# Affine steps on the bare rows: from pairs between the stages to single steps beside the weight loads, pinned on GpSimd

## The chip, the cores and the metric

One core of a Trainium2 chip runs the whole program. The metric is device time in microseconds (us) of one execution. The core has TensorE (PE, with its weight loads as PEld), VectorE (DVE), ScalarE (ACT), GpSimd (POOL) and SyncE (SP), which here issues every DMA from one queue. Each engine takes its instructions in the order in which the program lists them; semaphores hold an instruction until what it reads is there and what it overwrites has been read.

## The reference, cut to what matters

Two layers (`DEPTH = 2`) of a transformer on 512 rows (plus 256 context rows, 768 in all) of 1024 numbers. Each layer is feed-forward, mixer, feed-forward, and each of these ends in a residual with a layer norm:

```python
def swiglu(h, wg, wu, wd):
    return (jax.nn.silu(h @ wg) * (h @ wu)) @ wd

def sublayer_in(h, m, i):
    return h * (1.0 + m[..., i, 1, :]) + m[..., i, 0, :]

def residual(h, sub, m, i, g, b):
    return layer_norm(DEEPNORM_ALPHA * h + (1.0 + m[..., i, 2, :]) * sub, g, b)
```

The last step of `layer_norm` is an affine one, times `g` and plus `b` for each column. The hidden width of the feed-forward is 2816, which the kernel cuts into eleven pairs of 128 columns.

## The kernel before

Four feed-forward stages run, called here by layer and place: (0,0), (0,2), (1,0) and (1,2), with a mixer after (0,0) and one after (1,0). All four are one function, `ffn` (L367 to L851). Stage (1,2) has 512 rows, the others 768.

**Pairs and groups.** The eleven pairs are taken in five groups, [0,1], [2,3], [4,5], [6,7], [8,9,10] (L365). For each pair there are gate and up products (tiles `pl`, `pc` at L574 for pairs done plainly, `ch` and `sd` at L512 for the others), the result `act` (L450, L451), and at the end of each group `down` (L712), which multiplies `act` with the down weights into PSUM tiles `pd` (L723), two of them in turn, one for each of the six row tiles. ScalarE copies the first group's `pd` to `acc` (L729); VectorE adds the later groups (L731). The last group is done by `down_last`.

**Weights.** `prepare` (L817) pops jobs from a list: `load(pr, q)` brings the gate (q=0) or up (q=1) weights of a pair, `prep_down(pr)` the down weights, 1 MB each, into two buffers `raw` (L345). Every 128x512 part is then split into two fp16 pieces, the high one by ScalarE (L331), the rest by VectorE (L332). In the stages with 768 rows, pairs from 2 on are multiplied in seven products instead of eight, and for this `load` first makes four sums of the raw weights on GpSimd, `S1` to `S4` (L427 to L430); these take three buffers in turn, so `S4` waits until `S1` has been split. The pieces lie in a ring of 21 blocks that TensorE's products free again. In `load` the splits stand in the order raw, raw, `S2`, `S3`, `S1`, `S4`, raw.

**Affine steps.** A layer norm whose result goes into a feed-forward stage (0,2), (1,0) or (1,2) stores only the rows without gain and bias (`row`, "bare rows"). The residual at the end of that stage needs them with both. `dress` (L741) is a generator that does this in steps: for each half of the columns it loads gain and bias (`gx`, `bx`, L750, L751), and for each row tile it loads a 128x512 piece of `row` (`xd`, L754), multiplies and adds on GpSimd (L755, L756) and stores the result as `xrow` (L757). Twelve steps in (0,2) and (1,0), eight in (1,2). The tiles come from four buffers `bc`, which the gates of the residual (L737) use later too. `xrow` is read at the end, in `residual` (L768).

**What sets the order.** The kernel is written in one stream; a scheduler with a timeline of its own then orders each engine's instructions, and may put one that it takes to be ready ahead of others that stand before it in the source. In the source two affine steps stand after the `prepare` of each of the pairs 2 to 7 (L841). `ada_vec` (L154) is other work between the products: 1 MB loads `adaw` with one buffer (L169) and 16 small matmuls for each (L164), four loads for each of the vectors that a stage has in its list (six in (0,0) and (0,2), four in (1,0), none in (1,2)).

Of the kernel before, what the change touches and what calls it, by code (L numbers as in the profile page):

```python
# [11 lines left out]
ALU = mybir.AluOpType  # L12
# [30 lines left out]
def kernel(  # L43
# [5 lines left out]
    out, stop=None, out_ctx=None,  # L49
):  # L50
    nc = tc.nc
    V, A, G, PE = nc.vector, nc.scalar, nc.gpsimd, nc.tensor
# [314 lines left out]
    def ffn(l, i, uT, stream, ntiles, nxt, last, todo):  # L367
# [5 lines left out]
        with tc.tile_pool(name=f"ffn{l}{i}", bufs=1) as fp:  # L373
# [103 lines left out]
            def input_differences():  # L477
                new_differences()
                for t in range(ntiles // 2):
                    u = []  # L480
                    for q in range(2):
                        u.append(ft("xa", [P, KC, P], f"u{l}{i}{t}{q}"))
                        tq = t + q * ntiles // 2
                        nc.sync.dma_start(out=u[q], in_=(stream.whole[:, :, tq * P:(tq + 1) * P] if start else
                                                         stream.inputs[tq]))
                    differences(u[0][:, 0:4], u[1][:, 0:4], u[0][:, 4:8], u[1][:, 4:8], slice(0, 4),
                                slice(t * P, (t + 1) * P), [P, 4, P], f"{t}")
# [220 lines left out]
            def new_acc():  # L708
                for t in range(ntiles):
                    acc[t] = ft("xa", [P, D], f"acc{l}{i}_{t}")  # L710

            def down(gi, prs):  # L712

                for t in range(ntiles):
                    hf, o = t // (ntiles // 2), (t % (ntiles // 2)) * P
                    pp = big([P, 2, 512], f"pd{l}{i}_{gi}{t}")
                    for h in range(2):
                        pd = pp[:, h]
                        n = 0
                        for q in prs:  # L720
                            for cc in range(2):
                                for a, b in PASSES:
                                    PE.matmul(pd, lhsT=acts[q][2 * cc + hf][:, a, o:o + P],  # L723
                                              rhs=wd[q][2 * cc + h][:, b],
                                              start=(n == 0), stop=(n == len(prs) * 6 - 1))
                                    n += 1
                    pp = pp.rearrange("p h f -> p (h f)")
                    if gi == 0:
                        A.copy(acc[t], pp)  # L729
                    else:  # L730
                        V.tensor_tensor(out=acc[t], in0=acc[t], in1=pp, op=ALU.add)  # L731
# [9 lines left out]
            def dress():  # L741

                n = 3 * stream.prev[0] + stream.prev[1]
                bare = dict(stream.rows)
                for t in range(ntiles):
                    stream.rows[t] = dram.tile([P, D], F32, name=f"xrow{l}{i}_{t}")
                for h in range(2):
                    sl = slice(h * 512, (h + 1) * 512)
                    g, b = (ft("bc", [P, 512], f"{nm}{l}{i}{h}") for nm in ("gx", "bx"))
                    nc.sync.dma_start(out=g, in_=agb[n, sl].partition_broadcast(P))  # L750
                    nc.sync.dma_start(out=b, in_=agb[6 + n, sl].partition_broadcast(P))  # L751
                    for t in range(ntiles):
                        xt = ft("bc", [P, 512], f"xd{l}{i}_{t}{h}")
                        nc.sync.dma_start(out=xt, in_=bare[t][:, sl])  # L754
                        G.tensor_tensor(out=xt, in0=xt, in1=g, op=ALU.mult)  # L755
                        G.tensor_tensor(out=xt, in0=xt, in1=b, op=ALU.add)  # L756
                        nc.sync.dma_start(out=stream.rows[t][:, sl], in_=xt)  # L757
                        yield

            dressing = dress() if stream.bare else None  # L760

            def residual(h):

                sl = slice(h * 512, (h + 1) * 512)
                gates = gate_rows_of(h)
                for t in range(ntiles):
                    xt = ft("pt", [P, 512], f"xt{l}{i}_{t}{h}")
                    nc.sync.dma_start(out=xt, in_=stream.rows[t][:, sl])  # L768
                    if stream.prev is None:
                        A.mul(xt, xt, ALPHA)  # L770
                    c_ = acc[t][:, sl]
                    G.tensor_tensor(out=c_, in0=c_, in1=gates[0 if t < NLT else 1], op=ALU.mult)  # L772
                    V.tensor_tensor(out=c_, in0=c_, in1=xt, op=ALU.add)
# [40 lines left out]
            def need(job):  # L814
                return 7 if job[0] == load and job[1] not in gu_plain else 4

            def prepare(used=0):  # L817

                ahead[0] -= used
                while jobs and ahead[0] + need(jobs[0]) <= NBLOCK + NEXTRA:  # L820
                    job = jobs.pop(0)
                    ahead[0] += need(job)
                    job[0](*job[1:])

            if start:
                finish = first_pair()
            else:
                load_plain(0)
            prepare()
            for gi, prs in enumerate(GROUPS):  # L830
                for q in prs:
                    if start and q == 0:
                        finish()
                    else:
                        (gate_up_plain if q in gu_plain else gate_up)(q)
                    if q == 0 and not whole_plain:
                        input_differences()
                    if q == 1:
                        new_acc()
                    prepare(2 * need((load, q)) if q > 0 else 0)  # L840
                    for _ in range(2 if dressing and 1 < q < 8 else 0):  # L841
                        next(dressing, None)
                    if gi == len(GROUPS) - 1 and q < NPAIR - 1:
                        residual(q - prs[0])
                if gi < len(GROUPS) - 1:
                    down(gi, prs)
                    prepare(4 * len(prs))
# [769 lines left out]
    for n, (l, i) in enumerate(steps):  # L1617
        last = n == len(steps) - 1
        nxt = None if last else steps[n + 1]
        todo = list(plan.get((l, i), []))  # L1620
        if i == 1:
            norm = mixer(l, uT, stream, nxt, last)
        else:
            ntiles = NT if not (l == DEPTH - 1 and i == 2) else NLT
            norm = ffn(l, i, uT, stream, ntiles, nxt, last, todo)
        if not last:
            uT, stream = norm.uT, norm.stream
# [62 lines left out]
```

## Time and profile before

| | us |
|---|---|
| runs, median (lowest to highest of 3) | 2800.84 (2794.35 to 2801.38) |
| profiled execution | 2799.31 |
| its span, first to last instruction | 2797.5 |
| PE busy in it | 2666.7 (95%) |
| DVE, ACT, POOL busy | 1754.1 (63%), 1146.7 (41%), 839.9 (30%) |
| mean granted TensorE clock | 0.986 |

Busy time is the time in which an engine had an instruction of its own in work. A timeline lists instructions in order of time, merged where equal ones follow each other; in brackets stands how long the engine had been idle just before and what released it. All times below are counted from the start of the span.

### The profile page before, as it was taken

To read this page: it belongs to the slowest core of one execution; us is meant where nothing else is said; L and a number is where in the kernel's file an instruction comes from. 1 tells how busy PE (TensorE), PEld (TensorE's weight loads), DVE (VectorE), ACT (ScalarE), POOL (GpSimd) and SP (SyncE) were. 2 spreads that over 40 slices of the span, in tenths; PEclk is the share of its full clock that TensorE was granted. 3 is DMA by queue.
4 is the path that set the end of the run, shared out by engine and by line. 5 is a ranking of instruction groups with operands and counts; after the bars stand their busy time and mean duration, and the time that the engine had idled before them with its cause. 6 is when DMAs were issued, how large, how long until landed. Compare 5 with 4: busy or idle time off the path is not lost.

```text
span 2797.5 us, 42410 instructions
## 1 busy us (share of the span) xinstructions
PE 2666.7 (95%) x16703; PEld 1576.1 (56%) x16703; DVE 1754.1 (63%) x2705; ACT 1146.7 (41%) x2464; POOL 839.9 (30%) x798
## 2 busy tenths in 40 slices
PE   7999999999899997999999979999999899899998
PEld 4455455567677864554555535555556777744443
DVE  3665567776867674655576735656787777544455
ACT  2443334444437453433344423433544547443321
POOL 0331234232525226322340352315151525130011
PEclk9999999999999999999999989999999999999999
DMA  9453354233233253543453544432423333182330
GB/s 296 134 179 123 107 180 163 97 122 98 74 87 97 84 203 129 201 138 106 151 175 114 194 149 168 155 117 83 146 84 99 101 97 106 58 273 92 115 103 31
DMA packets 234494, 365.68 MB, mean 131 GB/s; under 512 B 16072, under 2 KB 168374, under 8 KB 234294
## 3 DMA queue, kind: packets, MB, share of 16 engines
q1 hardware_dynamic: 234294, 362.97, 39.5%
q8 instruction: 131, 2.15, 0.3%
q14 instruction: 69, 0.57, 0.1%
HBM read 312.96 MB, written 34.75 MB: 124 GB/s over the span
## 4 chain that ended last, share of the span: by engine, by line
PE 69%; DVE 9%; DMA 8%; ACT 4%; POOL 4%; issue 3%; SPq 2%; DVEq 0%; POOLq 0%; ACTq 0%
PE pd L723 15%; PE ch L512 13%; PE sd L512 10%; PE pl L574 7%; PE pd L792 5%; PE pm L1547 4%; PE ada L164 3%; PE px L947 2%; PE pkav L957 2%; PE pjaq L947 1%; PE pjak L947 1%; SPq L1248 1%; DMA xd<-row 1%; DMA adaw<-in_ada_w_dram 1%; DVE pcgu L332 1%
## 5 line engine op out<-in xcount | busy, mean ns | idle before, releaser
L512 PEld LDWEIGHTS <-pcgu 128*128 128x128 f16 x3444 | 333.3, 98 | 246.4 <-issue 29.0
L723 PE MATMUL pd<-pcd,act 128*128 128x512 f16 x1602 | 381.3, 382 | 7.6 <-DVE act L451 5.9
L723 PEld LDWEIGHTS <-act 128*128 128x128 f16 x2112 | 206.3, 99 | 284.2 <-issue 38.8
L574 PE MATMUL pl<-uT,pcgu 128*128 128x512 f16 (+2 forms) x1212 | 256.6, 367 | 4.8 <-ACT uT L222 4.6
L512 PE MATMUL ch<-T,pcgu 128*128 128x384 f16 x1476 | 255.8, 326 | 0.0
L574 PEld LDWEIGHTS <-pcgu 128*128 128x128 f16 x1692 | 162.9, 98 | 154.3 <-issue 13.0
L331 ACT ACTIVATE pcgu<-rawgu 128x512 f16<-128x512 f32 x222 | 136.7, 627 | 257.7 <-PE pd L723 96.1
L332 DVE SCALAR_TENSOR_TENSOR pcgu<-rawgu,pcgu 128x512 f16<-128x512 f32 x222 | 197.2, 901 | 60.8 <-ACT pcgu L331 60.1
L731 DVE TENSOR_TENSOR acc<-acc,pd 128x1024 f32<-128x1024 f32 x66 | 80.5, 1219 | 195.4 <-PE pd L723 195.4
L430 POOL TENSOR_TENSOR S4gu<-rawgu,S2gu 128x512 f32<-128x512 f32 x54 | 76.8, 1422 | 374.7 <-DVE pcgu L332 252.5
L723 PE MATMUL pd<-ped,act 128*128 128x512 f16 x510 | 137.3, 384 | 21.3 <-ACT acc L729 21.3
L512 PEld LDWEIGHTS <-pegu 128*128 128x128 f16 x1092 | 105.8, 98 | 85.9 <-issue 17.4
L427 POOL TENSOR_TENSOR S1gu<-rawgu 128x512 f32<-128x512 f32 x54 | 81.7, 1514 | 240.5 <-DMA rawgu<-in_ffn_w_gate_dram 122.0
L957 PEld LDWEIGHTS <-uT 128*128 128x128 f16 x1344 | 133.2, 99 | 25.6 <-issue 5.8
L236 ACT ACTIVATE u<-pt,abc 128x128 f32<-128x128 f32 x224 | 81.3, 468 | 152.6 <-PE pt L233 141.6
L792 PE MATMUL pd<-pcd,act 128*128 128x512 f16 x594 | 140.6, 379 | 0.0
L772 POOL TENSOR_TENSOR acc<-acc,gate 128x512 f32<-128x512 f32 x44 | 61.6, 1421 | 238.9 <-DVE acc L731 238.7
L93 POOL TENSOR_SCALAR rs<-mv 128x1 f32<-128x1 f32 x32 | 15.1, 473 | 392.5 <-DVE mv L281 392.5
L792 PEld LDWEIGHTS <-act 128*128 128x128 f16 x792 | 77.5, 98 | 89.3
L451 DVE TENSOR_TENSOR act<-sg,act 128x384 f16<-128x384 f32 (+1 forms) x172 | 122.6, 758 | 5.2 <-ACT act L450 5.2
L519 ACT COPY U<-ch 128x384 f32<-128x384 f32 x162 | 76.6, 473 | 114.3 <-PE ch L512 114.3
L332 DVE SCALAR_TENSOR_TENSOR pcd<-rawd,pcd 128x512 f16<-128x512 f32 x133 | 98.2, 749 | 40.1 <-ACT pcd L331 39.6
(365 smaller groups left out, 5303.0 us busy)
## 6 DMA issues: line engine op xcount, KB each, us to landing
adaw<-in_ada_w_dram SPq DMA_DIRECT2D x64, 1024.0 KB
rawd<-in_ffn_w_down_dram SPq DMA_DIRECT2D x44, 1024.0 KB
rawgu<-in_ffn_w_gate_dram SPq DMA_DIRECT2D x43, 1024.0 KB
rawgu<-in_ffn_w_up_dram SPq DMA_DIRECT2D x43, 1024.0 KB
rawwo<-in_w_out_dram SPq DMA_DIRECT2D x8, 1024.0 KB
row<-yh SPq DMA_DIRECT2D x16, 512.0 KB
xd<-row SPq DMA_DIRECT2D x32, 256.0 KB
xrow<-xd SPq DMA_DIRECT2D x32, 256.0 KB
```

The lines of the kernel that those rows point to most:

```text
L164: PE.matmul(pa[32 * j:32 * j + 32, :], lhsT=scT[:, k - 2 + q, :], rhs=raw[:, q, j * 256:(j + 1) * 256], start=(k == 2 and q == 0), stop=(k ...
L331: A.activation(pc[:, 0], src, AF.Copy, scale=SW)
L332: V.scalar_tensor_tensor(out=pc[:, 1], in0=src, scalar=SW, in1=pc[:, 0], op0=ALU.mult, op1=ALU.subtract)
L427: G.tensor_tensor(out=s1, in0=a21, in1=a22, op=ALU.add)
L451: V.tensor_tensor(out=pc[:, 1], in0=src, in1=pc[:, 0], op=ALU.subtract)
L512: PE.matmul(pp, lhsT=wt[pr_][q][m][:, a, k, :], rhs=rhs, start=(n == 0 and m in (1, 2, 5)), stop=(n == 11), skip_group_check=m in (1, 6, 7 ...
L574: PE.matmul(pp[:, j, o:o + hi - lo], lhsT=wp.at(a, k, cc * P, (cc + 1) * P), rhs=uT[:, b, k, lo:hi], start=(n == 0), stop=(n == KC * 3 - 1))
L723: PE.matmul(pd, lhsT=acts[q][2 * cc + hf][:, a, o:o + P], rhs=wd[q][2 * cc + h][:, b], start=(n == 0), stop=(n == len(prs) * 6 - 1))
L792: PE.matmul(pd, lhsT=acts[q][2 * cc + hf][:, a, o:o + P], rhs=wd[q][2 * cc + h][:, b], start=(n == 0), stop=(n == len(prs) * 6 - 1))
L947: PE.matmul(pp, lhsT=pc.at(a, k, cc * P, (cc + 1) * P), rhs=uT[:, b, k, lo:hi], start=(n == 0), stop=(n == KC * 3 - 1))
L957: PE.matmul(pp, lhsT=uT[:, a, k, t * P:(t + 1) * P], rhs=pc.at(b, k, 0, n_), start=(n == 0), stop=(n == KC * 3 - 1))
L1547: PE.matmul(pm[:, q * 256:(q + 1) * 256], lhsT=mT_[k // 4][:, a, k % 4, :], rhs=wo[2 * hf + q].at(b, k, 0, 256), start=(n == 0), stop=(n = ...
```

## The change

```diff
                     for t in range(ntiles):
                         xt = ft("bc", [P, 512], f"xd{l}{i}_{t}{h}")
                         nc.sync.dma_start(out=xt, in_=bare[t][:, sl])
-                        G.tensor_tensor(out=xt, in0=xt, in1=g, op=ALU.mult)
+                        tc.keep_in_program_order(G.tensor_tensor(out=xt, in0=xt, in1=g, op=ALU.mult))
                         G.tensor_tensor(out=xt, in0=xt, in1=b, op=ALU.add)
...
                     job = jobs.pop(0)
                     ahead[0] += need(job)
                     job[0](*job[1:])
+                    if dressing and job[0] == load and job[1] > 2:
+                        next(dressing, None)
...
                     prepare(2 * need((load, q)) if q > 0 else 0)
-                    for _ in range(2 if dressing and 1 < q < 8 else 0):
-                        next(dressing, None)
```

One affine step is now written behind each `load` of a pair from 3 on, so behind each gate and each up load, until the steps are used up. `keep_in_program_order` adds an edge for the scheduler: the multiplication stands on GpSimd behind the instruction that was written last for GpSimd, which in (0,2) and (1,0) is the `S4` of that load. It adds no wait on the chip. The work is the same; the instructions of PE, ACT and DVE stand as before but for a few exchanges of neighbours, and in (1,2) SP and POOL stand as before too. In (0,2) and (1,0), SP and POOL change.

On POOL, at the start of the products of pair 2 in stage (0,2), before (`S1gu_20` is the first sum of the gate weights of pair 2, `S1gu_21` of the up weights; `xd_20` is row tile 2, column half 0):

```order
L429 TENSOR_TENSOR S3gu_20_10866<-rawgu_20_10862 128x512
L755 TENSOR_TENSOR xd_20_11718<-xd_20_11718,gx_11397 128x512
L430 TENSOR_TENSOR S4gu_20_10867<-rawgu_20_10862,S2gu_20_10865 128x512
L755 TENSOR_TENSOR xd_30_11723<-xd_30_11723,gx_11397 128x512
L427 TENSOR_TENSOR S1gu_21_11051<-rawgu_21_11049 128x512
L756 TENSOR_TENSOR xd_20_11718<-xd_20_11718,bx_11398 128x512
L756 TENSOR_TENSOR xd_30_11723<-xd_30_11723,bx_11398 128x512
L428 TENSOR_TENSOR S2gu_21_11052<-S1gu_21_11051,rawgu_21_11049 128x512
L755 TENSOR_TENSOR xd_40_12241<-xd_40_12241,gx_11397 128x512
L755 TENSOR_TENSOR xd_50_12246<-xd_50_12246,gx_11397 128x512
L756 TENSOR_TENSOR xd_40_12241<-xd_40_12241,bx_11398 128x512
L756 TENSOR_TENSOR xd_50_12246<-xd_50_12246,bx_11398 128x512
```

The same place with the change:

```order
L430 TENSOR_TENSOR S4gu_20_10867<-rawgu_20_10862,S2gu_20_10865 128x512
L427 TENSOR_TENSOR S1gu_21_11051<-rawgu_21_11049 128x512
L428 TENSOR_TENSOR S2gu_21_11052<-S1gu_21_11051,rawgu_21_11049 128x512
L429 TENSOR_TENSOR S3gu_21_11053<-rawgu_21_11049 128x512
L430 TENSOR_TENSOR S4gu_21_11054<-rawgu_21_11049,S2gu_21_11052 128x512
L427 TENSOR_TENSOR S1gu_30_11082<-rawgu_30_11080 128x512
L428 TENSOR_TENSOR S2gu_30_11083<-S1gu_30_11082,rawgu_30_11080 128x512
L429 TENSOR_TENSOR S3gu_30_11084<-rawgu_30_11080 128x512
L430 TENSOR_TENSOR S4gu_30_11085<-rawgu_30_11080,S2gu_30_11083 128x512
L755 TENSOR_TENSOR xd_00_11121<-xd_00_11121,gx_11117 128x512
L756 TENSOR_TENSOR xd_00_11121<-xd_00_11121,bx_11118 128x512
L427 TENSOR_TENSOR S1gu_31_11363<-rawgu_31_11361 128x512
```

The affine steps that stood among the sums of pairs 2 and 3 have gone behind them: the first one now follows the last sum of the gate weights of pair 3, the others follow one by one behind later loads.

On SP, in stage (1,0), the end of the stretch of affine steps before (`gate` are the gates of the residual, `rawgu_31` the up weights of pair 3):

```order
L754 DMA xd_51_18089<-row_5_15001 128x512
L737 DMA gate_18586<-grow_2_12968 128x512
L757 DMA xrow_4_16130<-xd_41_18084 128x512
L757 DMA xrow_5_16131<-xd_51_18089 128x512
L737 DMA gate_18588<-grow_2_12968 128x512
L737 DMA gate_18871<-grow_2_12968 128x512
L737 DMA gate_18873<-grow_2_12968 128x512
L348 DMA rawgu_31_16081<-in_ffn_w_up_dram 128x8x256
L348 DMA rawd_2_16112<-in_ffn_w_down_dram 128x2x1024
```

On SP in the same stage with the change, from the gate weights of pair 2 on:

```order
L348 DMA rawgu_20_15597<-in_ffn_w_gate_dram 128x8x256
L348 DMA rawgu_21_15784<-in_ffn_w_up_dram 128x8x256
L348 DMA rawgu_30_15815<-in_ffn_w_gate_dram 128x8x256
L348 DMA rawgu_31_16096<-in_ffn_w_up_dram 128x8x256
L757 DMA xrow_0_15846<-xd_00_15856 128x512
L348 DMA rawd_2_16132<-in_ffn_w_down_dram 128x2x1024
L754 DMA xd_20_16453<-row_2_14802 128x512
L169 DMA adaw_5_2_15962<-in_ada_w_dram 128x2x1024
L757 DMA xrow_1_15847<-xd_10_16127 128x512
L348 DMA rawd_3_16408<-in_ffn_w_down_dram 128x2x1024
L754 DMA xd_30_16645<-row_3_14883 128x512
L169 DMA adaw_5_4_16028<-in_ada_w_dram 128x2x1024
```

The up weights of pair 3 no longer stand behind all twelve affine steps, but ahead of the first store. The stores and row loads now stand one by one among the later weight loads; 19 of the 40 `adaw` loads of (0,2) and (1,0) stand directly behind one of them (10 and 9), where before none did. The four loads of the residual's gates go from the end of the old stretch to the end of the new one, around the loads of pair 9.

## Rows read from the trace of the kernel before

**Rows 1.** The page, busy time: engine, us, share of the span, instructions

```profile
PE 2666.7 (95%) x16703; PEld 1576.1 (56%) x16703; DVE 1754.1 (63%) x2705; ACT 1146.7 (41%) x2464; POOL 839.9 (30%) x798
```

**Rows 2.** Windows: length, PE, PEld, DVE, ACT, POOL busy, clock, DMA: (0,0), (0,2), (1,0)

```profile
114.53:524.36 409.83, 406.03 (x2469) 214.05 (x2470) 241.59 (x334) 159.95 (x296) 114.32 (x79) 0.99 0.43 145
1070.93:1494.52 423.59, 408.72 (x2498) 215.18 (x2496) 246.76 (x337) 156.96 (x288) 140.82 (x100) 0.98 0.45 152
1606.73:2030.80 424.07, 401.49 (x2366) 213.13 (x2364) 243.22 (x328) 156.43 (x291) 143.10 (x100) 0.98 0.41 135
```

**Rows 3.** Timeline of PE, (0,2) and (1,0): start, us, what, count [idle before]

```profile
1074.25 2.98 PE L723 MATMUL pd<-pcd,act 128*128 128x512 f16 x13 [0.78 <-DVE act L451]
...
1096.13 1.44 PE L723 MATMUL pd<-ped,act 128*128 128x512 f16 x3 [13.72 <-ACT acc L729]
...
1102.91 0.81 PE L723 MATMUL pd<-ped,act 128*128 128x512 f16 x3
...
1108.09 0.81 PE L723 MATMUL pd<-ped,act 128*128 128x512 f16 x3
...
1611.21 2.98 PE L723 MATMUL pd<-pcd,act 128*128 128x512 f16 x13 [1.94 <-DVE act L451]
...
1626.99 1.44 PE L723 MATMUL pd<-ped,act 128*128 128x512 f16 x3 [7.62 <-ACT acc L729]
...
1634.57 0.81 PE L723 MATMUL pd<-ped,act 128*128 128x512 f16 x3
...
1659.99 3.38 PE L512 MATMUL sd<-uT,pcgu 128*128 128x384 f16 x12 [3.86 <-ACT acc L729]
1663.21 2.11 PE L512 MATMUL ch<-T,pcgu 128*128 128x384 f16 x12
1669.86 3.56 PE L512 MATMUL ch<-T,pegu 128*128 128x384 f16 x12 [4.54 <-ACT U L519]
```

**Rows 4.** Timeline of ACT: (0,2), then (1,0)

```profile
1085.14 0.63 ACT L331 ACTIVATE pcgu<-S3gu 128x512 f16<-128x512 f32 x1 [7.48 <-POOL S3gu L429]
...
1094.55 0.63 ACT L331 ACTIVATE pcgu<-S4gu 128x512 f16<-128x512 f32 x1 [6.16 <-POOL S4gu L430]
1095.09 1.91 ACT L729 COPY acc<-pd 128x1024 f32<-128x1024 f32 x2
...
1658.41 0.63 ACT L331 ACTIVATE pcgu<-S4gu 128x512 f16<-128x512 f32 x1 [8.76 <-POOL S4gu L430]
```

**Rows 5.** Timeline of POOL, (0,2): affine steps and the sums of pair 2

```profile
1066.71 1.27 POOL L755 TENSOR_TENSOR xd<-xd,gx 128x512 f32<-128x512 f32 x1 [8.03 <-DMA xd<-row]
...
1070.39 1.72 POOL L427 TENSOR_TENSOR S1gu<-rawgu 128x512 f32<-128x512 f32 x1
...
1093.26 1.26 POOL L430 TENSOR_TENSOR S4gu<-rawgu,S2gu 128x512 f32<-128x512 f32 x1
```

**Rows 6.** Timeline of SP's queue, (1,0): the up weights of pair 3

```profile
1660.02 0.38 SPq L348 DMA_DIRECT2D rawgu<-in_ffn_w_up_dram  x1
```

**Rows 7.** Timeline of POOL, (0,0), without affine steps: up weights of pair 2

```profile
109.13 1.59 POOL L427 TENSOR_TENSOR S1gu<-rawgu 128x512 f32<-128x512 f32 x1 [0.68 <-POOL S4gu L430]
...
116.97 1.65 POOL L430 TENSOR_TENSOR S4gu<-rawgu,S2gu 128x512 f32<-128x512 f32 x1 [2.90 <-DVE pcgu L332]
```

**Rows 8.** Waits of PE in the window of (0,0): us in total, times, longest

```profile
PE ada L164 <- DMA adaw<-in_ada_w_dram: 3.8, 2, 2.0
```

**Rows 9.** Window over pairs 2 and 3 of (0,2), columns as in rows 2

```profile
1119.00:1187.00 68.00, 68.00 (x467) 38.08 (x466) 42.70 (x60) 31.55 (x59) 21.78 (x15) 1.00 0.59 196
```

**Rows 10.** Timelines of POOL and DVE at the end of that window

```profile
1178.34 1.27 POOL L430 TENSOR_TENSOR S4gu<-rawgu,S2gu 128x512 f32<-128x512 f32 x1 [10.43 <-DVE pcgu L332]
...
1182.48 1.76 DVE L332 SCALAR_TENSOR_TENSOR pegu<-S1gu,pegu 128x512 f16<-128x512 f32 x1
1184.17 0.68 DVE L332 SCALAR_TENSOR_TENSOR pcgu<-rawgu,pcgu 128x512 f16<-128x512 f32 x1
```

**Rows 11.** Waits of SP's queue in the window of (0,2)

```profile
SPq L754 <- DMA xrow<-xd: 8.2, 7, 2.9
```

## The prediction, made before the changed kernel ran

> **What bounds the kernel now.** I read the page's busy times first: TensorE is busy for 95% of the span [rows 1], so only the stretches in which it stands still, or runs slowly, can be won. Then the windows over three like stages, each from the start of the down products of group 0 to the last group: (0,0), which has no affine steps, is idle for 409.83 - 406.03 = 3.80 us; (0,2) for 14.87; (1,0) for 22.58 [rows 2]. The timeline of TensorE puts nearly all of the surplus in a few holes at the start of the two stages that have affine steps [rows 3]: 0.78 and 13.72 us in (0,2), and 1.94, 7.62, 3.86 and 4.54 us in (1,0). The largest is released by ScalarE's copy of `pd` into `acc`. The reader should now follow ScalarE backwards. Its copy at 1095.09 comes straight behind the split of `S4` at 1094.55, for which it had stood idle 6.16 us waiting on GpSimd, and before that 7.48 us for `S3` [rows 4]. ScalarE takes its instructions in order, so the copies, with which the splits have nothing to do, wait too, and TensorE has only two `pd` tiles. On GpSimd, `S1` of the up weights of pair 2 starts at 1070.39 and `S4` only at 1093.26, 22.87 us later [rows 5]. In (0,0) the same two are 116.97 - 109.13 = 7.84 us apart [rows 7]. The order of GpSimd shows what lies between: affine steps, some of which wait for their own row loads, as the one at 1066.71 did for 8.03 us [rows 5]. In (1,0) this happens twice. At pair 3 ScalarE waits 8.76 us for `S4` [rows 4], and the up weights of that pair leave SP's queue only at 1660.02 [rows 6], behind the stores and row loads of the steps.
>
> **What the change removes.** With the steps behind the sums, the holes go if nothing else is late there. Holes: 0.78 + 13.72 = 14.50 us in (0,2), 1.94 + 7.62 + 3.86 + 4.54 = 17.96 us in (1,0), together 32.46 us [rows 3]. The products right behind a hole are slow as well, and that goes with it. The 24 products from 1102.91 to 1108.09 take 5.18 us; the 24 from 1096.13 took 6.78, the 24 from 1626.99 to 1634.57 took 7.58: 1.60 and 2.40 us more. The two sets of 12 behind the holes of pair 2 took 3.38 and 3.56 where the set at 1663.21 took 2.11: 1.27 and 1.45 us [rows 3]. That is 6.72 us. Sum removed: 32.46 + 6.72 = **39.2 us**.
>
> **What is late next.** In (0,2), take `S1` where it is now, at 1070.39, and (0,0)'s 7.84 us to `S4`: 1078.23, plus 1.65 for `S4`, 0.63 for its split and half of 1.91 for the first copy: 1081.5 [rows 4, 5, 7]. TensorE ends its first two `pd` tiles at 1096.13 - 13.72 = 1082.4, or 1081.6 without the wait of 0.78. So the copy is just in time, with almost no margin, if `S1` starts no earlier; without the steps ahead of it, it can. I take the hole as gone and keep its return as the first rival. The window check agrees: if both stages fell to the idle time of (0,0), they would give 11.07 + 18.78 = 29.9 us of idle and the 6.7 us of slow products, 36.6 in all [rows 2].
>
> **What it adds and moves.** Nothing is computed anew. (1,2) keeps its order on POOL and SP: 0. In (0,2) and (1,0), 24 steps move into the stretch in which TensorE stands still least. Each is two GpSimd instructions of 1.27 us [rows 5], 2.54 us. Queued behind them are the sums of the next load, and ScalarE and VectorE wait for those. The cover is the time that GpSimd waits anyway: 10.43 us before the `S4` at 1178.34 [rows 10], and GpSimd is busy for 21.78 of 68 us while TensorE is busy for all 68 [rows 9]. I cost them at 0 there; without that cover each costs up to 2.54 us. The moved gates of the residual come one to two pairs before their use: 0.
>
> Each step also issues a row load and a store on SP's queue. A store waits there for its addition, and a later row load for an earlier store to land, at most 2.9 us, 8.2 us over seven times [rows 11]. The weight loads behind them wait too. Those of pairs are issued well ahead; the 1 MB `adaw` loads have one buffer and little room. Stage (0,0), without any affine step, already loses 3.8 us on two of them, 2.0 at most [rows 8]. With the change 19 of 40 stand directly behind a row load or a store. Bounds: 0, since TensorE's place in its order gives each load some microseconds, and 19 x 2.0 = 38 us. A gain on this item is excluded, because nothing makes these loads earlier. I take 3.8 us, two stalls as in (0,0), since the queue waited for stores only about 1.2 us at a time.
>
> **A rule that speaks against the change.** A split on VectorE that reads two SBUF tiles took 1.76 us at 1182.48 and 0.68 us at 1184.17 [rows 10]; the longer one ran beside a GpSimd sum. The Trainium skill says in "GPSIMD Engine Reference", section "8. Key points", that GpSimd shares its SBUF interfaces with VectorE and that they contend when a VectorE instruction has two SBUF inputs. The trace agrees with it. By that rule the steps go from a stretch where VectorE mostly waits to one where it works. If each of the 48 GpSimd instructions held VectorE for 1.76 - 0.68 = 1.08 us on the path, that would be 51.8 us, and the sum +12.6 instead of -39.2. The row against it: VectorE is busy for 42.70 of the 68 us in which TensorE never stops although GpSimd's sums run beside it [rows 9]. So I give this little.
>
> **The sum.** 39.2 - 3.8 = 35.4 us less than the profiled execution's 2799.31 us: 2763.9. The median of the runs shown, 2800.84, lies 1.53 us above that execution, so the forecast for the median is **2765.4 us**.
>
> **Rivals.**
> 1. *The hole of group 0 comes back in part.* The copies still stand behind the split of `S4`, which waits for five VectorE splits behind the start of `S1`. If these run at 1.76 instead of 0.68 us because the sums now run without a break beside them, `S4` is 5 x 1.08 = 5.4 us later, and with some 2 us of slow products (1.60 and 2.40) each stage keeps 7.4 us. For it: the margin of 0.1 us worked out above. Against it: (0,0) runs the same chain without such a hole. Gain 35.4 - 14.8 = 20.6, time 2780.
> 2. *`adaw` loads late behind the stores.* Place: SP's queue from pair 2 on. It turns the gain into a loss from 39.2 / 19 = 2.06 us for each of the 19; at 2.5 us each, 47.5 - 39.2 = +8.3, time 2809. For it: the stalls of (0,0) with less in the queue. Against it: the longest stall there is 2.0 us, and the wait for a store is mostly shorter.
> 3. *VectorE held up by the moved steps*, the mechanism of the 1.08 us above: decides from 39.2 / 48 = 0.82 us for each GpSimd instruction on the path; 2799.31 + 12.6 + 1.53 = 2813.
> 4. *The wait only changes its name.* Pair 2 or 3 is held by its weights from HBM or by the ring, not by the sums: the 15 to 20 us won at group 0 are waited for there again, and the time stays near 2798. Against it: (0,0) has the same loads and ring and no such wait. That the change doesn't do what it says is excluded for the order, which shows the steps behind the sums in both stages.
>
> **How the numbers follow.** Forecast 0.70 (2756 to 2776: the 39.2 us in full and 5 us of run-to-run luck at the low end, 24 at the high end); more than that 0.03; rival 1 0.16; rival 2 0.03; rival 3 0.02; rival 4 0.06. The range 2756 to 2784 holds the forecast and most of rival 1. About 0.3%, 8.4 us, is what a measurement of this kernel can tell from no change. Faster by more: the forecast, the better case and rival 1, 0.89. Slower: 0.04, from rivals 2 and 3. Same: the rest, 0.07, rival 4 and the near edge of the others.
>
> **What would show it.** Right: in (0,2) and (1,0) no idle of TensorE above 2 us released by `acc`; `S1` to `S4` of the up weights of pair 2 some 8 us apart; the up weights of pair 3 issued before the first `xrow`; the idle time of both windows near 4 and 9 us. If rival 1 holds, a hole of some 5 us before the third `pd` tile stays. If rival 2 holds, many waits of L164 for `adaw` appear. Rival 3 would show as waits of TensorE for VectorE in pairs 4 to 8, rival 4 as waits at pair 2 or 3 for loads. The prediction is wrong if those windows shorten by less than 20 us together, or if a stage that the change leaves alone becomes longer.

## The result, and the profile after the change

The changed kernel takes 2759.19 us in the median (2758.19 to 2764.83), the kernel before 2797.6 in the same series (2793.06 to 2801.38). The ratio is 0.9864 with a 95% interval of 0.9851 to 0.9877. It is 38.4 us faster where 35.4 were forecast; the forecast of 2765.4 us for the median was 6.2 us too high, inside its range. Half of that is the starting value: the forecast began at 2800.84, the median of three runs, and with a fourth it is 2797.6.

The page's busy times, to be held against [rows 1]:

```profile
PE 2657.9 (96%) x16703; PEld 1574.1 (57%) x16703; DVE 1775.9 (64%) x2705; ACT 1147.2 (42%) x2464; POOL 855.5 (31%) x798
```

Nothing more is computed and nothing less: the counts of instructions are those of before. TensorE is busy 8.8 us less and the span is 41.1 us shorter, so 32.3 us of the difference is idle time. The windows over the three stages, cut at the same instructions and with the columns of [rows 2]:

```profile
113.27:519.93 406.66, 404.83 (x2469) 213.68 (x2470) 241.10 (x334) 160.03 (x296) 114.33 (x79) 1.00 0.44 146
1066.60:1473.68 407.08, 404.93 (x2498) 214.75 (x2496) 258.83 (x333) 154.13 (x284) 153.88 (x103) 1.00 0.48 160
1585.89:1988.71 402.82, 395.31 (x2366) 211.53 (x2364) 253.31 (x324) 153.44 (x284) 153.53 (x102) 1.00 0.44 144
```

The window of (0,2) is 423.59 - 407.08 = 16.5 us shorter, that of (1,0) 424.07 - 402.82 = 21.3 us, together 37.8. The remaining 3.3 us lie outside, 3.2 of them in (0,0), whose program is the same; over the runs below its length differs by as much with no change in it. So the gain of the medians, 38.4, is within a microsecond the gain of these two windows: 27.8 us less idle and 10.0 us less busy. Their idle times are 2.15 us and 7.51 us, where 14.87 and 22.58 stood. (0,2) is now as long as (0,0).

TensorE at the start of the down products of (0,2), where the holes of [rows 3] were. The last line is a new small wait in (1,0), 100 us later, at the down products of the second group:

```profile
1066.60 0.81 PE L723 MATMUL pd<-ped,act 128*128 128x512 f16 x3
...
1076.96 0.81 PE L723 MATMUL pd<-ped,act 128*128 128x512 f16 x3
...
1686.63 0.39 PE L723 MATMUL pd<-pcd,act 128*128 128x512 f16 x1 [0.25 <-DVE act L451]
```

The third `pd` tile begins at 1076.96, 10.36 us after the first, without a pause: two tiles of 5.18 us each. ScalarE in the same place, for [rows 4]:

```profile
1069.99 0.62 ACT L331 ACTIVATE pcgu<-S4gu 128x512 f16<-128x512 f32 x1
1071.98 1.01 ACT L729 COPY acc<-pd 128x1024 f32<-128x1024 f32 x1 [1.37 <-PE pd L723]
```

Read the bracket: the copy now waits for TensorE, 1.37 us, where before TensorE waited for the copy. GpSimd, for [rows 5], with the sums of the up weights of pair 2, the last sum of pair 3's gate weights, and the first affine step:

```profile
1055.26 1.26 POOL L427 TENSOR_TENSOR S1gu<-rawgu 128x512 f32<-128x512 f32 x1
1056.60 1.47 POOL L428 TENSOR_TENSOR S2gu<-S1gu,rawgu 128x512 f32<-128x512 f32 x1
1063.71 1.65 POOL L429 TENSOR_TENSOR S3gu<-rawgu 128x512 f32<-128x512 f32 x1 [5.64 <-DVE pegu L332]
1068.26 1.66 POOL L430 TENSOR_TENSOR S4gu<-rawgu,S2gu 128x512 f32<-128x512 f32 x1 [2.90 <-DVE pcgu L332]
...
1096.25 1.65 POOL L430 TENSOR_TENSOR S4gu<-rawgu,S2gu 128x512 f32<-128x512 f32 x1 [21.34 <-DVE pegu L332]
1097.86 1.71 POOL L755 TENSOR_TENSOR xd<-xd,gx 128x512 f32<-128x512 f32 x1
1099.65 1.60 POOL L756 TENSOR_TENSOR xd<-xd,bx 128x512 f32<-128x512 f32 x1
```

The first affine step comes behind a sum before which GpSimd had stood idle for 21.34 us. SP's queue in (1,0), for [rows 6]:

```profile
1614.33 0.37 SPq L348 DMA_DIRECT2D rawgu<-in_ffn_w_up_dram  x1
1620.57 0.34 SPq L757 DMA_DIRECT2D xrow<-xd  x1
```

The up weights of pair 3 leave 28.4 us after the first down product of the stage (1585.89), before the first store; in the kernel before it was 53.3 us (1660.02 against 1606.73).

What is new are waits of TensorE for `adaw`, in (0,2) and then in (1,0), for [rows 8] (us in total, times, longest):

```profile
PE ada L164 <- DMA adaw<-in_ada_w_dram: 1.9, 2, 1.2
...
PE ada L164 <- DMA adaw<-in_ada_w_dram: 2.7, 2, 1.5
```

SP's waits in the window of (0,2), for [rows 11]: the queue is held by stores that wait for GpSimd (L757) and by row loads that wait for a store (L754, 18.9 us in place of 8.2). First the stores in the kernel before, then both with the change:

```profile
SPq L757 <- POOL xd L756: 32.3, 9, 11.8
```

```profile
SPq L757 <- POOL xd L756: 51.9, 11, 9.4
...
SPq L754 <- DMA xrow<-xd: 18.9, 8, 4.9
```

### The profile page after: what moved, and what is told of

Its sections match the earlier page's. It is cut to its first block, busy times and chain, and to the rows that moved or that the text cites. A ratio compares the mean times of both kernels' runs of the same rounds, so it can differ in the third digit from the quotient of the medians.

```text
span 2756.4 us, 42388 instructions
## 1 busy us (share of the span) xinstructions
PE 2657.9 (96%) x16703; PEld 1574.1 (57%) x16703; DVE 1775.9 (64%) x2705; ACT 1147.2 (42%) x2464; POOL 855.5 (31%) x798
## 3 DMA queue, kind: packets, MB, share of 16 engines
q8 instruction: 131, 2.15, 0.3%
## 5 line engine op out<-in xcount | busy, mean ns | idle before, releaser
L512 PEld LDWEIGHTS <-pcgu 128*128 128x128 f16 x3444 | 333.5, 98 | 240.1 <-issue 21.3
L723 PE MATMUL pd<-pcd,act 128*128 128x512 f16 x1602 | 378.2, 380 | 5.7 <-DVE act L451 3.6
L723 PEld LDWEIGHTS <-act 128*128 128x128 f16 x2112 | 204.9, 98 | 257.2 <-issue 10.9
L512 PE MATMUL ch<-T,pcgu 128*128 128x384 f16 x1476 | 255.9, 326 | 0.0
L512 PEld LDWEIGHTS <-pegu 128*128 128x128 f16 x1092 | 105.3, 98 | 79.4 <-issue 10.4
L723 PE MATMUL pd<-ped,act 128*128 128x512 f16 x510 | 135.1, 379 | 0.1
L332 DVE SCALAR_TENSOR_TENSOR pegu<-rawgu,pegu 128x512 f16<-128x512 f32 x68 | 61.9, 915 | 97.7 <-ACT pegu L331 97.2
```

The source lines that it names most:

```text
L332: V.scalar_tensor_tensor(out=pc[:, 1], in0=src, scalar=SW, in1=pc[:, 0], op0=ALU.mult, op1=ALU.subtract)
L512: PE.matmul(pp, lhsT=wt[pr_][q][m][:, a, k, :], rhs=rhs, start=(n == 0 and m in (1, 2, 5)), stop=(n == 11), skip_group_check=m in (1, 6, 7 ...
L723: PE.matmul(pd, lhsT=acts[q][2 * cc + hf][:, a, o:o + P], rhs=wd[q][2 * cc + h][:, b], start=(n == 0), stop=(n == len(prs) * 6 - 1))
```

## The experiments

The table gives, for every kernel, the length of the windows over (0,2) and (1,0) from the first product of group 0's down to the first product of `down_last`, with TensorE's idle time in it. Then come the median time and the ratio to the kernel before in the same series.

| kernel | (0,2): us, idle | (1,0): us, idle | time | ratio, 95% interval |
|---|---|---|---|---|
| before | 385.09, 14.87 | 384.02, 21.20 | 2797.6 | |
| changed | 368.57, 2.15 | 363.18, 6.56 | 2759.19 | 0.9864 (0.9851-0.9877) |
| after_again | 370.21, 3.67 | 367.71, 9.58 | 2762.35 | 0.9875 (0.9856-0.9893) |
| pin_old | 369.15, 2.91 | 361.13, 5.24 | 2757.72 | 0.9851 (0.9834-0.9867) |
| pin_old_again | 367.54, 1.37 | 362.04, 6.14 | 2757.53 | 0.9856 (0.9838-0.9873) |
| move_free | 384.26, 13.85 | 382.95, 19.07 | 2798.77 | 1.0001 (0.9992-1.0011) |
| pin_first_only | 370.85, 2.83 | 382.49, 20.96 | 2782.09 | 0.9941 (0.9922-0.9959) |
| no_steps | 368.69, 0.42 | 360.26, 3.07 | 2753.70 | 0.9841 (0.9824-0.9857) |
| old_dma_only | 368.76, 0.49 | 360.34, 3.30 | 2756.91 | 0.9849 (0.9830-0.9868) |
| new_double | 380.92, 9.40 | 369.52, 11.65 | 2781.91 | 0.9941 (0.9922-0.9960) |
| new_side | 374.38, 5.83 | 366.07, 7.94 | 2771.69 | 0.9909 (0.9888-0.9929) |
| store_pool | 372.37, 3.85 | 367.33, 8.19 | 2769.95 | 0.9902 (0.9885-0.9919) |
| pin_old_store_pool | 374.69, 5.29 | 363.32, 6.46 | 2767.10 | 0.9888 (0.9867-0.9909) |
| late_affine | 379.11, 8.53 | 374.66, 14.69 | 2797.03 | 0.9994 (0.9983-1.0005) |

**after_again.** The changed kernel, unaltered.

> The changed kernel once more, so that the others can be held against it on one chip. All theories: 2759 us within 5, 38 us (1.36%) below the kernel before. In the window over stage (0,0), which the change does not touch, the first profile of the changed kernel stood idle 1.8 us and that of before 3.8; if that difference is the scatter of single executions, this one lies anywhere between 1 and 4.

2762.35 us, inside the 5 us. The window of (0,0) in the table's sense is 377.02 us long, that of the first profile 376.62, and 373.4 to 380.75 over all the runs here: single executions scatter by some microseconds there, and the idle time in it lies between 4.0 and 8.6 us (5.6 and 5.8 in the two profiles of the changed kernel, 7.8 before). The waits for `adaw` in (0,2) and (1,0) scatter as well: seven waits, 9.4 us, in this profile, four, 4.6 us, in the first.

**pin_old and move_free: which half of the change does it.**

```diff
 pin_old (against before; the steps stay at prepare of pairs 2 to 7)
-G.tensor_tensor(out=xt, in0=xt, in1=g, op=ALU.mult)
+tc.keep_in_program_order(G.tensor_tensor(out=xt, in0=xt, in1=g, op=ALU.mult))

 move_free (against the changed kernel; the step stays behind each load)
-tc.keep_in_program_order(G.tensor_tensor(out=xt, in0=xt, in1=g, op=ALU.mult))
+G.tensor_tensor(out=xt, in0=xt, in1=g, op=ALU.mult)
```

> Only the pin: the steps stay two at a time behind the preparing of pairs 2 to 7, as before, but are held behind the instruction of GpSimd that the program lists above them. Theory A (what counts is that no affine step stands ahead of a sum which is wanted earlier): the holes are gone, the windows over (0,2) and (1,0) within 3 us of the 407.1 and 402.8 us of the changed kernel, time 2757 to 2766. Rival B (it is the one-at-a-time cadence beside the loads): two steps in a row hold the sums by 5 us each time, at most half the gain is left, 2778 or more.

> Only the move: one step behind each load of pairs 3 and later, as in the changed kernel, but without the pin. Its instructions on GpSimd stand nearly as in the kernel before, all twelve steps of a stage among the sums of pairs 2 and 3. Theory A: no gain, 2793 to 2802, with the holes of about 13.7 and 7.6 us at the third down tile and those at pair 3 of (1,0) back. Rival B: the cadence in the program already brings part of the gain, below 2785.

pin_old has the whole gain, in both of its runs; move_free has none. GpSimd in pin_old, (0,2): the last sum of pair 2's up weights, and the first affine step, which now follows the sums of pair 3:

```profile
1073.25 1.66 POOL L430 TENSOR_TENSOR S4gu<-rawgu,S2gu 128x512 f32<-128x512 f32 x1 [2.90 <-DVE pcgu L332]
...
1113.72 1.77 POOL L755 TENSOR_TENSOR xd<-xd,gx 128x512 f32<-128x512 f32 x1
```

TensorE and GpSimd in move_free, (0,2):

```profile
1095.88 1.44 PE L723 MATMUL pd<-ped,act 128*128 128x512 f16 x3 [13.47 <-ACT acc L729]
```

```profile
1069.93 1.72 POOL L427 TENSOR_TENSOR S1gu<-rawgu 128x512 f32<-128x512 f32 x1
1071.62 3.25 POOL L756 TENSOR_TENSOR xd<-xd,bx 128x512 f32<-128x512 f32 x2
...
1089.34 2.48 POOL L755 TENSOR_TENSOR xd<-xd,gx 128x512 f32<-128x512 f32 x2 [4.34 <-DMA xd<-row]
1091.78 1.26 POOL L756 TENSOR_TENSOR xd<-xd,bx 128x512 f32<-128x512 f32 x1
1093.00 1.26 POOL L430 TENSOR_TENSOR S4gu<-rawgu,S2gu 128x512 f32<-128x512 f32 x1
```

It is the picture of [rows 3, 5] again, although the program lists each step far behind these sums: the scheduler lets an instruction whose inputs are there early stand early. The cadence in the source does nothing unless the order is held. Rival B falls on both sides. In its second run the pin alone was compared once more:

> pin_old once more on the chip of this series. If the pin alone is better than pin and move together, it stays 3 to 6 us below the changed kernel, 2754 to 2759; if the difference of 4.6 us was the scatter of a few executions, 2758 to 2764.

2757.53 us. The pin alone has been 1.5 to 4.8 us below the two runs of the changed kernel; the intervals of the ratios overlap, so that it is the better one is likely and not shown.

**pin_first_only: do the two stages add up.**

```diff
-tc.keep_in_program_order(G.tensor_tensor(...))
+(tc.keep_in_program_order if l == 0 else (lambda x: x))(G.tensor_tensor(...))
```

> The changed kernel with the pin in (0,2) alone; in (1,0) the steps float forward as before. If the two stages' gains add up, (0,2)'s window is 407 us as with the change and (1,0)'s 424 as before, and the time is the changed kernel's plus 21.2, 2780. If the holes of (1,0) come from something that (0,2) hands on, (1,0)'s window shortens too and the time is below 2772.

They do: 370.85 us in (0,2) and 382.49 in (1,0), in the table's windows (368.57 with the change, 384.02 before), and 2782.09 us. The holes of (1,0) are its own. TensorE there:

```profile
1607.76 1.44 PE L723 MATMUL pd<-ped,act 128*128 128x512 f16 x3 [7.54 <-ACT acc L729]
```

**old_dma_only: GpSimd's order or SP's queue.**

```diff
 (against before)
 nc.sync.dma_start(out=xt, in_=bare[t][:, sl])
-G.tensor_tensor(out=xt, in0=xt, in1=g, op=ALU.mult)
-G.tensor_tensor(out=xt, in0=xt, in1=b, op=ALU.add)
 nc.sync.dma_start(out=stream.rows[t][:, sl], in_=xt)
```

> The kernel before without the two GpSimd instructions of each step: the row loads and the stores stay on SP's queue, ahead of the weight loads of pairs 2 and 3 as before, so the bare rows are only copied and the gain and bias are missing in the residual. It parts GpSimd's share from that of SP's queue. Theory A1 (only GpSimd's order made the holes; the queue was late because its stores waited for GpSimd): windows of (0,2) and (1,0) near 407 and 403 us, 2755 to 2763. Rival D (SP's queue has a share of its own): the hole of 13.7 us goes, those at pair 3 of (1,0), 3.86 and 4.54 us, stay, the time 2767 to 2775.

2756.91 us, with windows of 368.76 and 360.34 us (368.57 and 363.18 with the change): all holes are gone, also the two of (1,0) that stood before products of pair 2 and came from the sums of pair 3. Theory A1 holds and rival D falls. In the trace of (0,2), all row loads and stores still stand ahead of the up weights of pair 3 on SP's queue:

```profile
1075.47 0.95 SPq L757 DMA_DIRECT2D xrow<-xd  x2
1076.52 0.91 SPq L348 DMA_DIRECT2D rawgu<-in_ffn_w_gate_dram  x1
1095.43 0.38 SPq L348 DMA_DIRECT2D rawgu<-in_ffn_w_up_dram  x1
```

These weights leave 28.4 us after the first down product (1066.99), as in the changed kernel; in the kernel before it was 44.8. So 24 transfers ahead of the weight loads harmed nothing here, where no store among them waited for GpSimd. On GpSimd the sums run without affine steps between them, `S1` of the up weights of pair 2 at 1060.58, `S4` at 1068.66:

```profile
1060.58 1.26 POOL L427 TENSOR_TENSOR S1gu<-rawgu 128x512 f32<-128x512 f32 x1 [1.87 <-DMA rawgu<-in_ffn_w_up_dram]
...
1068.66 1.66 POOL L430 TENSOR_TENSOR S4gu<-rawgu,S2gu 128x512 f32<-128x512 f32 x1 [2.90 <-DVE pcgu L332]
```

**no_steps: what the steps still cost.**

```diff
 (against the changed kernel)
-dressing = dress() if stream.bare else None
+dressing = None
```

> The affine steps are left out altogether, with their row loads and stores: the residual reads the bare rows, so the layer norm's gain and bias are missing there. It shows what the steps still cost where the change has put them. Theory A (hidden, apart from the weight loads late behind stores): 0 to 5 us below the changed kernel, 2754 to 2760. Rival C (the moved steps still cost, through VectorE or through SP's queue): 10 us or more below it, under 2750, and the waits for the conditioning weights in the windows of (0,2) and (1,0), 1.9 and 2.7 us, go to nearly 0.

2753.70 us, 5.5 us below the changed kernel's first series and 8.7 below after_again, which ran in the same series: between Theory A's bound of 5 and rival C's 10. In (0,2) the changed kernel loses nothing against it in the first profile (368.57 and 368.69 us) and 1.5 us in the second. In (1,0) it loses 2.9 us in the first profile and 7.5 in the second. Of the waits for `adaw` in the two windows 0.3 us are left here, as rival C had it, but they are worth less than they look: in (0,2) TensorE's records at L164 are 29.17 us long in the changed kernel and 31.01 here, which sets 1.84 us against the 1.9 us of waits.

**new_double and new_side: has the place that the steps moved to room.**

```diff
 new_double (against the changed kernel): the bias subtracted and added again
 G.tensor_tensor(out=xt, in0=xt, in1=b, op=ALU.add)
+G.tensor_tensor(out=xt, in0=xt, in1=b, op=ALU.subtract)
+G.tensor_tensor(out=xt, in0=xt, in1=b, op=ALU.add)

 new_side (against the changed kernel): pinned products behind the store, on a tile of their own
 nc.sync.dma_start(out=stream.rows[t][:, sl], in_=xt)
+for q in (0, 256, 0, 256):
+    tc.keep_in_program_order(G.tensor_tensor(out=junk, in0=g[:, q:q + 256],
+                                             in1=b[:, q:q + 256], op=ALU.mult))
```

> The changed kernel with four GpSimd instructions a step in place of two (the bias is subtracted and added once more): 64 more instructions of some 1.5 us each, 96 us of work on GpSimd beside the same products. Theory A (the stretch has cover): 2758 to 2766. Rival 3 of the prediction (each GpSimd instruction holds VectorE by 1.08 us on the path): 64 x 1.08 = 69 us more, 2828; a third of them would give 2782.

> The changed kernel with four more GpSimd products of 128x256 behind each step, on a tile that nobody reads. As in the doubled run, GpSimd works more and reads two SBUF tiles each time, but no store waits for it. It parts the 20 us of the doubled run. If they came by the stores that are late on SP's queue (conditioning weights late, and the slower clock behind such a wait): 2760 to 2767. If they came by the sums behind the extra work and by VectorE beside it: 2776 to 2786.

The doubled steps cost 19.6 to 22.7 us (2781.91), with GpSimd busy 39.0 us longer in the window of (0,2) (192.89 against 153.88). The work on the side, 47.0 us longer there, cost 9.3 to 12.5 (2771.69), between the two expectations. So the place does not hold twice the work. That 2782 is also what a third of rival 3's price would give is no proof of that rival: in the two windows of new_double TensorE waits first of all for `adaw`, 7.2 + 3.3 = 10.5 us, against 3.8 in new_side and 4.6 with the change. Nor do the two runs part GpSimd's work from the late stores. In new_side no store reads the extra tile, but the next affine step stands behind the extra products on GpSimd, and SP's stores wait longer for GpSimd than in new_double. Over the whole span, first new_double, then new_side (123.7 with the change):

```profile
SPq L757 <- POOL xd L756: 137.9, 27, 9.6
```

```profile
SPq L757 <- POOL xd L756: 154.8, 28, 10.3
```

How the price divides between the two stays open. The waits of TensorE for `adaw` in the window of (0,2) and three windows around the longest of them, in new_double (columns as in [rows 2], the last but two is the granted clock; the second window is the start of the third):

```profile
PE ada L164 <- DMA adaw<-in_ada_w_dram: 7.2, 4, 3.1
```

```profile
1275.00:1317.00 42.00, 39.57 (x221) 19.21 (x218) 25.97 (x24) 12.15 (x23) 20.99 (x13) 1.00 0.26 89
1317.69:1322.00 4.31, 4.31 (x24) 1.78 (x25) 1.69 (x4) 0.00 (x0) 0.00 (x0) 0.50 0.96 318
1317.69:1345.00 27.31, 27.31 (x179) 14.73 (x180) 16.49 (x24) 10.65 (x20) 6.22 (x5) 0.89 0.71 241
```

Behind the wait of 3.12 us for `adaw` the granted clock is 0.50, the lower of its two levels (1.2 of 2.4 GHz), for 4.31 us, and 0.89 in the mean of 27.31 us: by estimate another 0.11 x 27.31 = 3.0 us, so this wait is paid twice. Not every wait is: behind the one of 2.70 us, at 1230.00 in the same trace, the clock is 1.00 over the next 27 us. In new_side TensorE's longest wait is for VectorE, with one for `adaw` behind it:

```profile
1225.06 0.81 PE L512 MATMUL ch<-uT,pcgu 128*128 128x384 f16 x4 [1.96 <-DVE sg L523]
1227.06 1.70 PE L164 MATMUL ada<-adaw,scT 128*32 128x256 f32 x16 [1.20 <-DMA adaw<-in_ada_w_dram]
```

**store_pool and pin_old_store_pool: is it the stores on SP's queue.**

```diff
 (against the changed kernel, and against pin_old)
-nc.sync.dma_start(out=stream.rows[t][:, sl], in_=xt)
+nc.gpsimd.dma_start(out=stream.rows[t][:, sl], in_=xt)
```

> The changed kernel with one difference: the store of each dressed half row is issued by GpSimd, right behind its own addition, and no longer by SP. Then no weight load on SP's queue stands behind a wait for GpSimd; the row loads stay on SP. Theory C1 (what the steps still cost in the changed kernel, 5.6 us over the version without them, is the conditioning weights late behind the stores): the waits for these weights in (0,2) and (1,0), 4.6 to 9 us in the two profiles of the changed kernel, fall below 2 us, time 2752 to 2758. Rival C2 (it is the traffic of the row loads and stores, or their issue on GpSimd costs the sums as much): waits and time as with the change, 2758 to 2764.

> As the run before, but with the steps two at a time where the old program had them, and pinned (pin_old with the stores on GpSimd's queue). Theory C1: 2750 to 2757, no more than the version without any steps within 3 us. Rival C2: as pin_old, 2755 to 2760.

Both are slower than without it, by 7.6 to 10.8 us and 9.4 to 9.6 us. Neither expectation came true: with no store on SP's queue the waits for `adaw` in store_pool are still 3.7 us in (0,2) and 4.5 in (1,0), and the time lies above the range of rival C2 too. SP's waits over the whole span, first in the changed kernel, then in store_pool, and the stores by their issuing queue in the same two:

```profile
SPq L757 <- POOL xd L756: 123.7, 28, 12.9
...
SPq L754 <- DMA xrow<-xd: 43.3, 18, 5.5
```

```profile
SPq L754 <- DMA xrow<-xd: 103.7, 21, 8.8
```

```profile
xrow<-xd SPq DMA_DIRECT2D x32, 256.0 KB, 2.0
```

```profile
xrow<-xd POOLq DMA_DIRECT2D x32, 256.0 KB, 3.9
```

A store issued by GpSimd lands 3.9 us after its issue, not 2.0. The next row load, which needs the buffer that the store frees, waits for it at the head of SP's queue, and the weight loads behind it wait as before: the wait of L757 has become one of L754. That would explain why nothing was won; how the 8 to 11 us divide between this and GpSimd's issuing was not tried. So these runs do not settle what the steps still cost, since the queue is still held for the stores. The transfers alone are not it, at least in their old place: with them and without GpSimd's instructions the windows are 368.76 and 360.34 us (old_dma_only), without both 368.69 and 360.26 (no_steps).

**late_affine: no steps, but the affine in the residual.**

```diff
 (against the changed kernel; dressing = None, g and b loaded next to the gates)
 nc.sync.dma_start(out=xt, in_=stream.rows[t][:, sl])
+G.tensor_tensor(out=xt, in0=xt, in1=g, op=ALU.mult)
+G.tensor_tensor(out=xt, in0=xt, in1=b, op=ALU.add)
 G.tensor_tensor(out=c_, in0=c_, in1=gates[...], op=ALU.mult)
 V.tensor_tensor(out=c_, in0=c_, in1=xt, op=ALU.add)
```

> The two GpSimd instructions are done in the residual itself, on the row that it loads anyway, behind pairs 8 and 9: no step, 32 row loads and 32 stores fewer. If the stores ahead of the conditioning weights are all that the steps still cost, up to 5 us below the changed kernel, 2754 to 2759. Against it: 24 instructions of a stage come behind the last sums, just ahead of GpSimd's share of the norm at the stage's end; if they end too late, the last stretch waits some 10 us in each of three stages, 2770 to 2790.

2797.03 us: the whole gain is lost, more than was expected against it. The windows of the table are 10.5 and 11.5 us longer than with the change; most of the rest lies behind them, at the ends of the stages. It is not the norm that TensorE waits for there. VectorE and TensorE at the end of (0,2); L781 is the residual's addition:

```profile
1455.34 1.74 DVE L781 TENSOR_TENSOR acc<-acc,xt 128x512 f32<-128x512 f32 x1 [2.38 <-POOL xt L778]
...
1465.66 1.75 DVE L781 TENSOR_TENSOR acc<-acc,xt 128x512 f32<-128x512 f32 x1
1467.34 3.62 DVE L451 TENSOR_TENSOR act<-sg,act 128x384 f16<-128x384 f32 x3
1470.88 0.68 DVE L781 TENSOR_TENSOR acc<-acc,xt 128x512 f32<-128x512 f32 x1
1471.48 0.54 DVE L451 TENSOR_TENSOR act<-sg,act 128x384 f16<-128x384 f32 x1
```

```profile
1473.75 2.72 PE L512 MATMUL sd<-T,pcgu 128*128 128x384 f16 x8 [5.10 <-DVE sg L537]
```

VectorE's additions wait for GpSimd's affine, and its instructions with two SBUF inputs are slow while GpSimd works: 1.75 us against 0.68 for the same addition, 3.62 / 3 = 1.21 against 0.54 for `act`. `sg` of L537 stands behind all of these on VectorE, and TensorE waits 5.10 us for it. This is the mechanism of the prediction's third rival, in a place where TensorE then waits for VectorE.

## Why the prediction was right

**What bounds the kernel.** The chain that it read out of [rows 3 to 5] is the cause, and this is shown: taking only the GpSimd instructions away (old_dma_only), or only holding them behind the sums (pin_old), removes all the holes that [rows 3] shows; moving them in the program without holding them (move_free) brings none of it. The two stages are independent (pin_first_only). Two of the signs came true as they were written: no idle of TensorE is released by `acc`, and the up weights of pair 3 leave before the first `xrow`. The idle times of the windows, 2.15 and 7.51 us, came out below the 4 and 9 that were named.

**Removed: 39.2 us.** Of the 32.46 us of holes none is left. The slow products at the down weights were taken at 1.60 and 2.40 us; L723's busy time in the two windows fell from 129.26 to 127.50 and from 129.87 to 127.48 us, 1.76 and 2.39. That they go with the hole is seen in the granted clock of the kernel before, behind the hole of 13.72 us:

```profile
1096.13:1102.91 6.78, 6.78 (x24) 2.74 (x24) 0.76 0.35 118
1102.91:1108.09 5.18, 5.18 (x25) 2.35 (x24) 1.00 0.40 143
```

The two sets at pair 2 were taken at 2.72 us; L512 lost 3.23 us in (1,0), and another 0.69 in (0,2) that the prediction did not have.

**Added: 3.8 us, two stalls.** There were four in this profile, 4.6 us, and seven in the next, 9.4 us. The size of one was mostly right (2.0 at most was said; the longest were 1.5 and 3.69). The net price against no_steps is 2.8 us in the one profile (368.57 + 363.18 against 368.69 + 360.26) and 9.0 in the other. The term lies between the two, and that it comes so near is in part luck. It was sized by row loads that wait for a store, 1.2 us at a time [rows 11], and left out the stores' own waits for GpSimd, which were 32.3 us in the window of (0,2) already before, up to 11.8 at a time, and are 51.9 now. A stall is also worth less than its length: L164's records in the two windows are 1.84 and 1.22 us shorter than before. And the two instructions of the first step took 1.71 + 1.60 = 3.31 us, not 2.54; the cover was enough for that as well.

**Where it failed in a detail.** "S1 to S4 of the up weights of pair 2 some 8 us apart" did not come true: 13.00 us in (0,2) and 9.5 in (1,0). The margin of 0.1 us, on which the first rival stood, was worked out with `S1` at its old place, 0.5 us before the first down product. It starts 11.3 us before it now, because the steps ahead of it are gone too, and it can afford its sums' waits for VectorE (5.64 and 2.90 us). The prediction had said that it could start earlier and put no number on it, so with hindsight the first rival got more weight (0.16) than the kernel gave it reason for.

**The rivals.** The first did not come: there is no hole at the third `pd` tile. The second is real but small, as above. The third is real as well: VectorE's busy time over the window of (0,2) is

```profile
1070.31:1439.00 368.69, 368.27 (x2266) 192.20 (x2264) 216.43 (x289) 135.83 (x247) 113.95 (x79) 1.00 0.43 143
```

in no_steps, and with the same 289 instructions 233.31 us in the changed kernel and 249.49 in new_double. That is 16.9 us for 24 GpSimd instructions of the steps and 33.1 us for 48, 0.70 and 0.69 us each. It is no constant: in pin_old, with the same counts, it is 226.23 us and 0.41 each. The prediction took 1.08 us and asked whether it lies on the path. At 24 instructions a stage it hardly does (368.57 and 370.21 us in the two profiles, 368.69 without); at 48 the window is 12.4 us longer than with 24, and 7.2 of its 9.40 us of idle are waits for `adaw`. The rule of the Trainium skill that the prediction weighed, "GPSIMD Engine Reference", section "8. Key points", that GpSimd and VectorE share SBUF interfaces and contend when VectorE has two SBUF inputs, agrees with these rows. What the contention cost depended here on the place: in late_affine TensorE waited 5.10 us for VectorE behind it. The fourth rival did not come.

## What to carry to other kernels

Where a scheduler orders an in-order engine by what is ready, work with early inputs and a late use is put ahead of work that others wait for; look for the engine that stands still behind it (here ScalarE's copies behind a split that waited for GpSimd), and hold the early work behind the sums with one constraint. Moving the source lines did nothing by itself here. Before putting work "under cover", look at the cover of all engines that share with it: here VectorE's slack in the middle of the stage hid what the same instructions cost in full at the stage's end.

## What had not been expected of the hardware

- GpSimd's work lengthens VectorE's: 0.70 us of VectorE's time for each 128x512 GpSimd instruction of two SBUF inputs in the changed kernel, 0.41 in pin_old, from windows of (0,2) with equal counts of VectorE's instructions.
- A short stall can be paid again in the clock: behind 3.12 us of waiting the granted clock was 0.50 over 4.31 us and 0.89 over 27.31 us, behind 13.72 us it was 0.76 over 6.78 us; behind 2.70 us it stayed at 1.00 (new_double, before).
- A store of 256 KB from GpSimd's queue landed after 3.9 us, from SP's after 2.0 us (medians of 32).
- 24 row loads and stores ahead of the weight loads of pair 3 on SP's queue cost nothing in old_dma_only, where no store among them waited for GpSimd.
